# Gated linear attention: the state carried over tiles of 128 frames, decays measured from the middle of a tile

## The chip, the cores and the metric

The kernel runs on one core of one Trainium2 chip. The metric is device time of one execution, in microseconds. A core has five engines that run beside each other and meet at semaphores: TensorE (PE) multiplies matrices and writes to PSUM; its weight loads are shown apart, as PEld. VectorE (DVE) and ScalarE (ACT) do elementwise work and read PSUM. GpSimd (POOL) does small elementwise work here and issues DMAs, also those that add to their target. SyncE (SP) issues most weight loads.

## The reference

One layer over 512 frames of 1024 channels: three branches of the normalised input, merged by gates, an output product, and an MLP. The change touches the first branch alone, the gated linear attention (GLA) with four heads of 64 key and 128 value channels, in chunks of 64 frames:

```python
b = jnp.cumsum(log_a.reshape(B, N, CHUNK, H, DK).astype(f32), axis=2)
e_pos = jnp.exp(b)
e_neg = jnp.exp(-b)
q_pos = qc * e_pos
a_causal = jnp.einsum('bnthd,bnshd->bnhts', q_pos, kc * e_neg)
a_anti = jnp.einsum('bnthd,bnshd->bnhts', qc * e_neg, kc * e_pos)
attn = jnp.where(lower, a_causal, a_anti)
o_intra = jnp.einsum('bnhts,bnshv->bnthv', attn, vc)
chunk_kv = jnp.einsum('bnshd,bnshv->bnhdv', kc * jnp.exp(b_last - b), vc)
chunk_decay = jnp.exp(b_last[:, :, 0])
...
def step(state, inp):
    kv, dec = inp
    return state * dec[..., None] + kv, state
...
o_inter = jnp.einsum('bnthd,bnhdv->bnthv', q_pos, prev)
return (o_intra + o_inter).reshape(B, S, H, DV).astype(v.dtype)
```

A frame reads every frame of its own chunk, with a decay by the distance in time, and all earlier chunks through a state that decays channel by channel. Only differences of `b` enter the result, so `b` may be counted from any point.

## The kernel before

**Layout.** Frames are cut into NT = 4 tiles of P = 128, so a tile holds two chunks. Two heads share one group of 128 partitions: head h = 2j + e sits in the 64 rows of half e of pair j. The queries qpos, qneg are zero in the other half, so a score matmul over all 128 rows gives one head.

**Products.** The large products split each fp32 operand into a rounded part and a remainder and add three products; that is `mm3`, lines 155 to 157. A weight tile is loaded by SyncE, rounded by ScalarE (`whi`, L145), its remainder is made on VectorE (`wlo`, L146). Where a weight is the sum of two, a POOL DMA adds the second to the first (L940 in the gate stage, L130 and L132 for sums kept in DRAM, which wait for a cast that paces them). The GLA's own products are plain fp32.

**Order.** The order of TensorE is written by hand: `weave` runs a list of GLA steps and deals 64 steps of other products between them (the output gates `gla_g`, the late fox gates `fox_late`), three matmuls of 512 columns each. The list is decays, key_turn, gla_scores, states, gla_scores, gla_values twice, then the second pair of heads, with gla_turn for the finished heads. The other engines' order is made by a planner that times the program.

**GLA step by step, for a pair j.**
- `decays` (L741): four matmuls of the log decays with `tri64`, a triangle inside each chunk, give `b` in PSUM. VectorE takes each chunk's last column (`bl`) and subtracts it (`ek`); ScalarE makes four exponentials: `ek`, `ep`, `en`, `dec`. VectorE makes kd = k·ek first, then kp, qpos, kn, qneg.
- `key_turn` (L770): four transposes of kd. Rows of even chunks go to kdE (VectorE), of odd chunks to kdO (ScalarE); the other halves are zero, from two memsets on POOL.
- `states` (L778): per chunk and head a matmul of 64 columns of kdE or kdO with the values, 16 in two PSUM banks; the two heads of a chunk use the two column halves of the array. VectorE scans over seven states.
- `gla_scores` (L798): eight matmuls per head, then eight copies under a mask (`msk_s`: same chunk and s ≤ t; same chunk and s > t) into `at`, which POOL sets to zero before.
- `gla_values` (L811): per head and tile the scores with the values, 128 columns (L818), and per chunk the queries with the state before the chunk, 64 columns (L824). In the first tile the scores' product is cut into two of 64 columns (L822). Then the norm of the head.
- `gla_turn` (L835): four transposes, times the output gate.

**Behind it** the gate products (`gate_group`) run, whose left factors are sums made by `lefts_2` (x at L920 and L921, then f2h and f2l at L922 and L923), and whose results are added into `ct` by `vec` (L949).

Of the kernel before, what the change touches and what calls it, by code (L numbers as in the profile page):

```python
# [9 lines left out]
F32 = mybir.dt.float32  # L10
# [54 lines left out]
def hybrid_block(ctx, tc, chunks, wst, memT, xN, cols, gffn, gfin, wup, cst, out):  # L65
    nc = tc.nc
# [5 lines left out]
    def nm(s):  # L72
        uid[0] += 1
        return f"{s}_{uid[0]}"
# [13 lines left out]
    def at_(shape=None):  # L88
        return pa.tile(shape or [P, 512], F32, tag="a", name=nm("a"))
# [161 lines left out]
    with pool("front") as fp:  # L251
# [101 lines left out]
        for k in range(KT):  # L353
# [3 lines left out]
            if k in (3, 5):  # L357
                h = k // 5
# [366 lines left out]


    with pool("gla") as lp:
        NC = 8
        qpos = [lp.tile([P, S], F32, name=f"qpos{e}") for e in range(2)]
        qneg = [lp.tile([P, S], F32, name=f"qneg{e}") for e in range(2)]  # L730
        kdE = lp.tile([P, NT, P], F32, name="kdE")
        kdO = lp.tile([P, NT, P], F32, name="kdO")
# [5 lines left out]
        nc.gpsimd.memset(kdO[0:64], 0.0)  # L738
        gs = {}

        def decays(j):  # L741
            pb = at_()
            for t in range(NT):
                nc.tensor.matmul(pb[:, t * P:(t + 1) * P], la[:, t, j * P:(j + 1) * P], tri64, start=True, stop=True)
            ep = lp.tile([P, S], F32, tag="ep", name=nm("ep"))
            en = lp.tile([P, S], F32, tag="en", name=nm("en"))
            bl = small(lp, NC, "bl").rearrange("p (c o) -> p c o", o=1)
            dec = small(lp, NC, "dec")
            ek = lp.tile([P, NC, 64], F32, tag="ek", name=nm("ek"))
            pb3 = pb.rearrange("p (c t) -> p c t", c=NC)  # L750
# [4 lines left out]
            nc.scalar.activation(en, pb, AF.Exp, scale=-1.0)  # L755
# [3 lines left out]
            kd = lp.tile([P, S], F32, tag="kd", name=nm("kd"))  # L759
            kd_ins = nc.vector.tensor_tensor(kd, gkT[j], ek.rearrange("p c t -> p (c t)"), op=ALU.mult).ins  # L760
            with tc.issue_after(kd_ins):
                nc.vector.tensor_tensor(kn, gkT[j], en, op=ALU.mult)
                nc.vector.tensor_tensor(kp, gkT[j], ep, op=ALU.mult)
                for e in range(2):
                    a = slice(64 * e, 64 * e + 64)
                    nc.vector.tensor_tensor(qpos[e][a], gqT[j][a], ep[a], op=ALU.mult)
                    nc.vector.tensor_tensor(qneg[e][a], gqT[j][a], en[a], op=ALU.mult)
            gs["d", j] = dec, kn, kp, kd

        def key_turn(j):  # L770
            kd = gs["d", j][3]
            pk = at_([P, NT, P])
            for t in range(NT):
                nc.tensor.transpose(pk[:, t, :], kd[:, t * P:(t + 1) * P], ident)
            nc.vector.tensor_copy(kdE[0:64], pk[0:64])
            nc.scalar.copy(kdO[64:128], pk[64:128])

        def states(j):  # L778
            dec = gs["d", j][0]
            prev = gs["s", j] = lp.tile([P, NC, P], F32, tag="prev", name=nm("prev"))  # L780
            for g in range(2):
                pv = at_([P, 4, P])
                for i in range(4):
                    c = 4 * g + i
                    t = c // 2
                    for e in range(2):
                        h = 2 * j + e
                        nc.tensor.matmul(pv[64 * e:64 * e + 64, i, :], (kdO if c % 2 else kdE)[:, t, 64 * e:64 * e + 64],
                                         gv[:, t, h * P:(h + 1) * P], start=True, stop=True)
                for i in range(4):  # L790
                    c = 4 * g + i
                    if c == 0:
                        nc.vector.tensor_copy(prev[:, 1, :], pv[:, 0, :])
                    elif c < NC - 1:
                        nc.vector.scalar_tensor_tensor(prev[:, c + 1, :], prev[:, c, :], dec[:, c:c + 1], pv[:, i, :],
                                                       op0=ALU.mult, op1=ALU.add)

        def gla_scores(h):  # L798
            j, e = divmod(h, 2)
            _, kn, kp, _ = gs["d", j]  # L800
            pc, pn = at_([P, NT, P]), at_([P, NT, P])
            at = gs["a", h] = lp.tile([P, NT, P], F32, tag="at", name=nm("at"), bufs=2)
            nc.gpsimd.memset(at, 0.0)
            for m, (ps, kk, qq) in enumerate(((pc, kn, qpos[e]), (pn, kp, qneg[e]))):
                for t in range(NT):
                    sl = slice(t * P, (t + 1) * P)
                    nc.tensor.matmul(ps[:, t, :], kk[:, sl], qq[:, sl], start=True, stop=True)
                for t in range(NT):
                    nc.vector.copy_predicated(at[:, t, :], msk_s[:, m, :], ps[:, t, :])

        def gla_values(h):  # L811
            j, e = divmod(h, 2)
            at, prev = gs["a", h], gs["s", j]
            po = at_([P, NT, P])
            for t in range(NT):
                vt = gv[:, t, h * P:(h + 1) * P]
                if t:
                    nc.tensor.matmul(po[:, t, :], at[:, t, :], vt, start=True, stop=False)  # L818
                for c in (2 * t, 2 * t + 1):
                    r = slice(64 * (c % 2), 64 * (c % 2) + 64)  # L820
                    if t == 0:
                        nc.tensor.matmul(po[r, t, :], at[:, t, r], vt, start=True, stop=c == 0)  # L822
                    if c:
                        nc.tensor.matmul(po[r, t, :], qpos[e][:, 64 * c:64 * c + 64], prev[:, c, :], start=False,  # L824
                                         stop=True)
# [578 lines left out]
def layout(inputs):  # L1404
# [3 lines left out]
    x = np.asarray(inputs["x"])[0]  # L1408
# [3 lines left out]
    for i, c in enumerate(chunks):  # L1412
# [4 lines left out]
        elif c[0] == "B":  # L1417
            _, q, h, (kh, ch) = c
            j = 8 * q + 4 * h + int(kh) - 1
# [9 lines left out]
        elif c[0] == "F":  # L1429
            _, q, h, (kh, ch) = c  # L1430
            ks = slice(512 * (int(kh) - 1), 512 * int(kh))
            for n in range(2):
                j = 8 * q + 4 * h + 2 * n + int(ch) - 1
# [4 lines left out]
        else:  # L1438
            g = wst[i].reshape(P, KT, P)
# [58 lines left out]
```

## Time and profile before

| | us |
|---|---|
| median of the runs | 843.53 |
| the runs | 843.0, 843.53, 901.48 |
| span of the profiled execution | 841.1 |
| ScalarE busy, whole span | 461.6 (55%) |
| DMA moved | 155.61 MB, mean 185 GB/s |

The profile is of one execution; its span runs from the first instruction to the last, and the run's time has what lies around it as well. Busy time is the share in which an engine holds an instruction: matmuls are pipelined, so a row's length on TensorE is longer than its step, and the start of the next row tells what it cost. An idle engine costs nothing as long as another is what the end waits for.

### The profile page before, as it was taken

What the parts mean: (1) busy time and instruction counts of PE and PEld (TensorE: products, weight loads), DVE (VectorE), ACT (ScalarE), POOL (GpSimd) and SP (SyncE); (2) the same over time, 40 slices, a digit from 0 to 9 for tenths busy, and PEclk for the clock granted to TensorE, in tenths of its full rate; (3) what the DMA queues carried; (4) which work ended last, traced back from release to release, by engine and by line L of the source; (5) the groups of instructions that cost most, each with busy time, mean ns of one, the idle gap of its engine ahead of it and who ended that gap; (6) DMA issues with size and microseconds to landing.
All of it is one profiled execution on the core that took longest, in us unless ns stands there. A gap on an engine that the chain in (4) does not pass through costs nothing.

```text
span 841.1 us, 12612 instructions
## 1 busy us (share of the span) xinstructions
PE 824.4 (98%) x4841; PEld 720.5 (86%) x4841; DVE 612.4 (73%) x954; ACT 461.6 (55%) x723; POOL 106.5 (13%) x129
## 2 busy tenths in 40 slices
PE   8999999999999999999999999999999999999995
PEld 6788888888888787988999889998998899889984
DVE  4856888665565686894686757896689678877897
ACT  6765777553345232543345435875577467646754
POOL 1001000001002110131431300011001100110011
PEclk9999999999999999999999999999999999999998
DMA  9424444448779582689986522968857975895543
GB/s 332 173 100 162 154 137 150 124 145 217 214 251 250 151 250 69 161 214 273 250 215 214 181 79 63 289 179 201 246 181 166 220 234 173 186 248 196 151 86 115
DMA packets 39181, 155.61 MB, mean 185 GB/s; under 512 B 4880, under 2 KB 5840, under 8 KB 37072
## 3 DMA queue, kind: packets, MB, share of 16 engines
q1 hardware_dynamic: 27712, 95.54, 31.9%
q0 software_dynamic: 9328, 54.01, 30.6%
q10 hardware_dynamic: 2080, 5.26, 1.8%
q8 instruction: 38, 0.62, 0.3%
q14 instruction: 23, 0.19, 0.1%
HBM read 152.65 MB, written 31.49 MB: 219 GB/s over the span
## 4 chain that ended last, share of the span: by engine, by line
PE 50%; DVE 2%; DMA 2%; issue 1%; ACT 0%; POOLq 0%; POOL 0%; ACTq 0%
PE mm L157 13%; PE mm L156 13%; PE mm L155 13%; PE a L156 4%; PE a L155 4%; PE a L157 4%; DMA wb<-in_wst_dram 2%; DVE h L1168 1%; PE a L1115 0%; DVE wlo L146 0%; ACT whi L145 0%; DVE h L1295 0%; DVE lo L209 0%; DVE h L1292 0%; DVE R L1165 0%
## 5 line engine op out<-in xcount | busy, mean ns | idle before, releaser
L155 PE MATMUL mm<-uhi,whi 128*128 128x512 f32 (+1 forms) x352 | 127.0, 361 | 0.8 <-ACT whi L145 0.8
L157 PE MATMUL mm<-uhi,wlo 128*128 128x512 f32 (+1 forms) x352 | 124.8, 354 | 1.0 <-DVE wlo L146 1.0
L156 PE MATMUL mm<-ulo,whi 128*128 128x512 f32 (+1 forms) x352 | 124.3, 353 | 0.0
L146 DVE TENSOR_TENSOR wlo<-raw,whi 128x1024 fp32r<-128x1024 f32 x68 | 91.5, 1349 | 34.7 <-ACT whi L145 34.4
L145 ACT CAST whi<-raw 128x1024 fp32r<-128x1024 f32 x68 | 71.2, 1049 | 65.1 <-PE mm L156 39.0
L208 ACT CAST hi<-raw 128x1024 fp32r<-128x1024 f32 x65 | 68.2, 1050 | 47.4 <-PE mm L156 34.3
L209 DVE TENSOR_TENSOR lo<-raw,hi 128x1024 fp32r<-128x1024 f32 x65 | 79.5, 1223 | 18.6 <-ACT hi L208 18.6
L157 PEld LDWEIGHTS mm<-uhi,wlo 128*128 128x128 f32 x352 | 67.2, 191 | 10.5 <-DVE wlo L146 1.4
L155 PEld LDWEIGHTS mm<-uhi,whi 128*128 128x128 f32 x352 | 67.4, 192 | 10.2 <-ACT whi L145 1.2
L156 PEld LDWEIGHTS mm<-ulo,whi 128*128 128x128 f32 x352 | 67.4, 192 | 8.0
L208 ACT CAST hi<-b 128x1024 fp32r<-128x1024 f32 x40 | 41.9, 1048 | 41.4 <-PE mm L157 26.8
L157 PE MATMUL mm<-u2h,lo 128*128 128x256 f32 x224 | 63.4, 283 | 0.0
L156 PE MATMUL mm<-u2l,hi 128*128 128x256 f32 x224 | 63.4, 283 | 0.0
L156 PE MATMUL mm<-lo,ch 128*128 128x512 f32 x160 | 62.5, 391 | 0.9 <-DVE lo L209 0.9
L155 PE MATMUL mm<-u2h,hi 128*128 128x256 f32 x224 | 63.4, 283 | 0.0
L157 PE MATMUL mm<-hi,cl 128*128 128x512 f32 x160 | 62.3, 389 | 0.0
L155 PE MATMUL mm<-hi,ch 128*128 128x512 f32 x160 | 62.3, 389 | 0.0
L209 DVE TENSOR_TENSOR lo<-b,hi 128x1024 fp32r<-128x1024 f32 x40 | 48.8, 1222 | 18.2 <-ACT hi L208 18.2
L1352 POOL DMA_DIRECT2D b<-in_wst_dram x32 | 27.4, 855 | 272.4 <-DVE lo L209 209.3
L155 PE MATMUL mm<-u2sh,hi 128*128 128x256 f32 x168 | 47.5, 283 | 0.0
L156 PE MATMUL mm<-u2sl,hi 128*128 128x256 f32 x168 | 47.5, 283 | 0.0
L157 PE MATMUL mm<-u2sh,lo 128*128 128x256 f32 x168 | 47.5, 283 | 0.0
(413 smaller groups left out, 2156.3 us busy)
## 6 DMA issues: line engine op xcount, KB each, us to landing
raw<-in_wst_dram SPq DMA_DIRECT2D x114, 512.0 KB
b<-in_wst_dram POOLq DMA_DIRECT2D x32, 512.0 KB, 5.4
raw<-T SPq DMA_DIRECT2D x28, 512.0 KB
T<-in_wst_dram POOLq DMA_DIRECT2D x12, 1024.0 KB, 8.9
b<-in_wst_dram SPq DMA_DIRECT2D x16, 512.0 KB
wb<-in_wst_dram POOLq DMA_DIRECT2D x15, 512.0 KB, 5.9
wb<-in_wst_dram SPq DMA_DIRECT2D x8, 512.0 KB
T<-in_wst_dram POOLq DMA_DIRECT2D x6, 512.0 KB, 5.2
```

Source lines behind the costliest of these rows:

```text
L145: cast = nc.scalar.copy(hi, raw)
L146: low_now[0] = nc.vector.tensor_tensor(lo, raw, f(hi), op=ALU.subtract).ins
L155: nc.tensor.matmul(ps, lh, rh, start=start, stop=False)
L156: nc.tensor.matmul(ps, lh, rl, start=False, stop=False)
L157: nc.tensor.matmul(ps, ll, rh, start=False, stop=stop)
L208: nc.scalar.copy(hi, src)
L209: return nc.vector.tensor_tensor(lo, src, f(hi), op=ALU.subtract).ins
L1168: nc.vector.tensor_tensor(to, to, x, op=op)
L1352: nc.gpsimd.dma_start(to[i], wst[index["B", q, i, x]], accum_op=ALU.add)
```

## The change

The state is now kept at the middle of each tile of 128 frames instead of the start of each chunk of 64. `b` is counted from frame 63 of a tile, backwards and forwards; column 63 of the product, which would be zero, is used for the sum from the tile's start to its middle. With the next tile's such sum, the last column gives the decay from one middle to the next (`end`, `dec`). The exponentials of both signs are written into one tile `ex`, and POOL sets column 63 of both to 1. kn now serves the scores and the states; kd, ek, kdE and kdO are gone. The first mask covers the whole tile (s ≤ t), so the scores of a tile's second chunk with its first one are read in `at`; the states are read per tile. The matmuls of the scores are as before.

```diff
-    ident, ones, tri, tri64 = (cst_s[:, i * P:(i + 1) * P] for i in range(4))
+    ident, ones, tri, mids = (cst_s[:, i * P:(i + 1) * P] for i in range(4))
...
-        nc.gpsimd.memset(kdE[64:128], 0.0)
-        nc.gpsimd.memset(kdO[0:64], 0.0)
...
-            nc.vector.tensor_copy(bl, pb3[:, :, 63:64])
-            nc.vector.tensor_tensor(ek, pb3, bl.to_broadcast([P, NC, 64]), op=ALU.subtract)
-            nc.scalar.activation(ek, ek, AF.Exp, scale=-1.0)
+            nc.scalar.activation(en, pb, AF.Exp, scale=-1.0)
+            nc.vector.tensor_copy(end, pb3[:, :NT - 1, P - 1:])
+            nc.vector.tensor_tensor(end, end, pb3[:, 1:, 63:64], op=ALU.add)
             nc.scalar.activation(ep, pb, AF.Exp)
-            nc.scalar.activation(en, pb, AF.Exp, scale=-1.0)
-            nc.scalar.activation(dec, bl.rearrange("p c o -> p (c o)"), AF.Exp)
+            nc.scalar.activation(dec, end.rearrange("p c o -> p (c o)"), AF.Exp)
+            nc.gpsimd.memset(ex.rearrange("p i t c -> p (i t) c")[:, :, 63:64], 1.0)
...
-            kd_ins = nc.vector.tensor_tensor(kd, gkT[j], ek.rearrange("p c t -> p (c t)"), op=ALU.mult).ins
-            with tc.issue_after(kd_ins):
-                nc.vector.tensor_tensor(kn, gkT[j], en, op=ALU.mult)
+            kn_ins = nc.vector.tensor_tensor(kn, gkT[j], en, op=ALU.mult).ins
+            with tc.issue_after(kn_ins):
                 nc.vector.tensor_tensor(kp, gkT[j], ep, op=ALU.mult)
...
-            for t in range(NT):
-                nc.tensor.transpose(pk[:, t, :], kd[:, t * P:(t + 1) * P], ident)
-            nc.vector.tensor_copy(kdE[0:64], pk[0:64])
-            nc.scalar.copy(kdO[64:128], pk[64:128])
+            for t in range(NT - 1):
+                nc.tensor.transpose(pk[:, t, :], kn[:, t * P:(t + 1) * P], ident)
+            kt = gs["k", j] = lp.tile([P, NT - 1, P], F32, tag="kt", name=nm("kt"))
+            nc.scalar.copy(kt, pk[:, :NT - 1, :])
...
+            for t in range(NT - 1):
+                for e in range(2):
+                    h = 2 * j + e
+                    nc.tensor.matmul(pv[64 * e:64 * e + 64, t, :], kt[:, t, 64 * e:64 * e + 64], gv[:, t, h * P:(h + 1) * P],
+                                     start=True, stop=True)
+            for t in range(NT - 1):
+                x = pv[:, t, :]
+                if t:
+                    x = mid[:, 0, :]
+                    nc.vector.tensor_tensor(x, mid[:, t, :], pv[:, t, :], op=ALU.add)
+                nc.vector.tensor_scalar(mid[:, t + 1, :], x, dec[:, t:t + 1], None, op0=ALU.mult)
...
             for t in range(NT):
-                vt = gv[:, t, h * P:(h + 1) * P]
+                nc.tensor.matmul(po[:, t, :], at[:, t, :], gv[:, t, h * P:(h + 1) * P], start=True, stop=t == 0)
                 if t:
-                    nc.tensor.matmul(po[:, t, :], at[:, t, :], vt, start=True, stop=False)
-                for c in (2 * t, 2 * t + 1):
-                    r = slice(64 * (c % 2), 64 * (c % 2) + 64)
-                    if t == 0:
-                        nc.tensor.matmul(po[r, t, :], at[:, t, r], vt, start=True, stop=c == 0)
-                    if c:
-                        nc.tensor.matmul(po[r, t, :], qpos[e][:, 64 * c:64 * c + 64], prev[:, c, :], start=False,
-                                         stop=True)
+                    nc.tensor.matmul(po[:, t, :], qpos[e][:, t * P:(t + 1) * P], mid[:, t, :], start=False, stop=True)
...
-    cst[:, 3 * P:4 * P] = np.where(same & (s <= t), 1.0 / 16.0, 0.0)
-    cst[:, 4 * P:5 * P] = same & (s <= t)
+    half = np.where(s < 64, -1.0 * (t < 63) * (s > t) + 1.0 * (t == 63), 1.0 * (s <= t) * (t > 63))
+    cst[:, 3 * P:4 * P] = half / 16.0
+    cst[:, 4 * P:5 * P] = s <= t
```

More of the change, by code (lines that the diff above doesn't have):

```diff
@@ L727, in hybrid_block @@
     with pool("gla") as lp:
-        NC = 8
         qpos = [lp.tile([P, S], F32, name=f"qpos{e}") for e in range(2)]
         qneg = [lp.tile([P, S], F32, name=f"qneg{e}") for e in range(2)]
-        kdE = lp.tile([P, NT, P], F32, name="kdE")
-        kdO = lp.tile([P, NT, P], F32, name="kdO")
         for e in range(2):
@@ L743, in decays @@
             for t in range(NT):
[L744 to L750, printed above, removed]
-            nc.vector.tensor_copy(bl, pb3[:, :, 63:64])
-            nc.vector.tensor_tensor(ek, pb3, bl.to_broadcast([P, NC, 64]), op=ALU.subtract)
-            nc.scalar.activation(ek, ek, AF.Exp, scale=-1.0)
+                nc.tensor.matmul(pb[:, t * P:(t + 1) * P], la[:, t, j * P:(j + 1) * P], mids, start=True, stop=True)
+            pb3 = pb.rearrange("p (t c) -> p t c", t=NT)
+            ex = lp.tile([P, 2, NT, P], F32, tag="ex", name=nm("ex"))
+            ep, en = (ex[:, i].rearrange("p t c -> p (t c)") for i in range(2))
+            dec = small(lp, NT - 1, "dec")
+            end = small(lp, NT - 1, "end").rearrange("p (c o) -> p c o", o=1)
+            nc.scalar.activation(en, pb, AF.Exp, scale=-1.0)
+            nc.vector.tensor_copy(end, pb3[:, :NT - 1, P - 1:])
+            nc.vector.tensor_tensor(end, end, pb3[:, 1:, 63:64], op=ALU.add)
             nc.scalar.activation(ep, pb, AF.Exp)
-            nc.scalar.activation(en, pb, AF.Exp, scale=-1.0)
-            nc.scalar.activation(dec, bl.rearrange("p c o -> p (c o)"), AF.Exp)
+            nc.scalar.activation(dec, end.rearrange("p c o -> p (c o)"), AF.Exp)
+            nc.gpsimd.memset(ex.rearrange("p i t c -> p (i t) c")[:, :, 63:64], 1.0)
             kn = lp.tile([P, S], F32, tag="kn", name=nm("kn"))
             kp = lp.tile([P, S], F32, tag="kp", name=nm("kp"))
-            kd = lp.tile([P, S], F32, tag="kd", name=nm("kd"))
-            kd_ins = nc.vector.tensor_tensor(kd, gkT[j], ek.rearrange("p c t -> p (c t)"), op=ALU.mult).ins
-            with tc.issue_after(kd_ins):
-                nc.vector.tensor_tensor(kn, gkT[j], en, op=ALU.mult)
+            kn_ins = nc.vector.tensor_tensor(kn, gkT[j], en, op=ALU.mult).ins
+            with tc.issue_after(kn_ins):
                 nc.vector.tensor_tensor(kp, gkT[j], ep, op=ALU.mult)
@@ L767, in decays @@
                     nc.vector.tensor_tensor(qneg[e][a], gqT[j][a], en[a], op=ALU.mult)
-            gs["d", j] = dec, kn, kp, kd
+            gs["d", j] = dec, kn, kp
         def key_turn(j):
-            kd = gs["d", j][3]
+            kn = gs["d", j][1]
             pk = at_([P, NT, P])
-            for t in range(NT):
-                nc.tensor.transpose(pk[:, t, :], kd[:, t * P:(t + 1) * P], ident)
-            nc.vector.tensor_copy(kdE[0:64], pk[0:64])
-            nc.scalar.copy(kdO[64:128], pk[64:128])
+            for t in range(NT - 1):
+                nc.tensor.transpose(pk[:, t, :], kn[:, t * P:(t + 1) * P], ident)
@@ L778, in states @@
+            kt = gs["k", j] = lp.tile([P, NT - 1, P], F32, tag="kt", name=nm("kt"))
+            nc.scalar.copy(kt, pk[:, :NT - 1, :])
         def states(j):
[L779 to L796, printed above, removed]
+            dec, kt = gs["d", j][0], gs["k", j]
@@ new lines, in states @@
+            mid = gs["s", j] = lp.tile([P, NT, P], F32, tag="mid", name=nm("mid"))
+            pv = at_([P, NT, P])
+            for t in range(NT - 1):
[9 more added lines that the diff above has]
+                nc.vector.tensor_scalar(mid[:, t + 1, :], x, dec[:, t:t + 1], None, op0=ALU.mult)
@@ L798, in gla_scores @@
         def gla_scores(h):
             j, e = divmod(h, 2)
-            _, kn, kp, _ = gs["d", j]
+            _, kn, kp = gs["d", j]
             pc, pn = at_([P, NT, P]), at_([P, NT, P])
@@ L812, in gla_values @@
             j, e = divmod(h, 2)
-            at, prev = gs["a", h], gs["s", j]
+            at, mid = gs["a", h], gs["s", j]
             po = at_([P, NT, P])
             for t in range(NT):
-                vt = gv[:, t, h * P:(h + 1) * P]
+                nc.tensor.matmul(po[:, t, :], at[:, t, :], gv[:, t, h * P:(h + 1) * P], start=True, stop=t == 0)
                 if t:
-                    nc.tensor.matmul(po[:, t, :], at[:, t, :], vt, start=True, stop=False)
-                for c in (2 * t, 2 * t + 1):
-                    r = slice(64 * (c % 2), 64 * (c % 2) + 64)
-                    if t == 0:
-                        nc.tensor.matmul(po[r, t, :], at[:, t, r], vt, start=True, stop=c == 0)
-                    if c:
-                        nc.tensor.matmul(po[r, t, :], qpos[e][:, 64 * c:64 * c + 64], prev[:, c, :], start=False,
-                                         stop=True)
+                    nc.tensor.matmul(po[:, t, :], qpos[e][:, t * P:(t + 1) * P], mid[:, t, :], start=False, stop=True)
             sq = lp.tile([P, NT, P], F32, tag="sq", name=nm("sq"))
```

## The prediction

> **What bounds the kernel now.** I read the page first, then the busy times by stage, the waits, and the timeline of TensorE where the diff works. In the page, PE is the matmul side of TensorE, PEld its weight loads.
>
> ```profile
> span 841.1 us, 12612 instructions
> ...
> PE 824.4 (98%) x4841; PEld 720.5 (86%) x4841; DVE 612.4 (73%) x954; ACT 461.6 (55%) x723; POOL 106.5 (13%) x129
> ```
>
> TensorE is busy for 98% of the span. That is an average, so I asked for the stages: the stretch of the gated linear attention (265 to 336 us), a part of its end, and the gate products behind it. Columns: length, busy time and instructions of PE, PEld, DVE, ACT and POOL, granted clock, share of the DMA engines, GB/s.
>
> ```profile
> 265.00:336.00 71.00, 71.00 (x450) 56.61 (x449) 48.72 (x114) 20.75 (x32) 12.59 (x19) 1.00 0.58 174
> 320.00:335.00 15.00, 15.00 (x91) 10.81 (x90) 7.67 (x21) 2.74 (x4) 2.04 (x2) 1.00 0.11 36
> 336.00:420.00 84.00, 82.03 (x549) 75.76 (x548) 59.92 (x58) 35.33 (x43) 24.60 (x23) 0.98 0.88 227
> ```
>
> In the attention's stage PE is never idle, VectorE is busy for 49 of 71 us and ScalarE for 21. So here the end is set by how long TensorE needs for its list, which is written out by hand, and a shorter list should shorten the kernel. In the list stand the attention's matmuls between 64 "fill" steps of gate projections (L155 to L157). But busy is not work. The waits of the weight loads in the same stage show gaps that no other engine causes ("issue"; total, times, longest):
>
> ```profile
> PEld a L818 <- issue: 1.7, 10, 0.2
> PEld a L822 <- issue: 1.4, 4, 0.4
> ```
>
> Both lines are in gla_values. The timeline of its first head shows what they are (start, length, engine, line, shape, count):
>
> ```profile
> 288.37 0.39 PE L157 MATMUL mm<-uhi,wlo 128*128 128x512 f32 x1
> 288.69 0.44 PE L822 MATMUL a<-gv,at 128*64 128x128 f32 x4
> 288.96 0.38 PE L824 MATMUL a<-prev,qpos 128*64 128x128 f32 x2
> 289.28 0.49 PE L818 MATMUL a<-gv,at 128*128 128x128 f32 x2
> 289.69 0.44 PE L824 MATMUL a<-prev,qpos 128*64 128x128 f32 x4
> 290.06 0.49 PE L818 MATMUL a<-gv,at 128*128 128x128 f32 x2
> ...
> 291.27 0.44 PE L824 MATMUL a<-prev,qpos 128*64 128x128 f32 x4
> 291.64 0.50 PE L155 MATMUL mm<-uhi,whi 128*128 128x512 f32 x1
> ```
>
> Each fp32 matmul has two records. The shape changes between 64 columns (128\*64) and 128 at every row, and the two records of L818 take 0.41 us to the next start. The scores, all of one shape, show the price without changes:
>
> ```profile
> 284.52 0.39 PE L157 MATMUL mm<-uhi,wlo 128*128 128x512 f32 x1
> 284.75 1.05 PE L807 MATMUL a<-qpos,kn 128*128 128x128 f32 x8
> 285.64 1.06 PE L807 MATMUL a<-qneg,kp 128*128 128x128 f32 x8
> 286.45 0.47 PE L155 MATMUL mm<-uhi,whi 128*128 128x512 f32 x1
> ```
>
> Eight matmuls (16 records) from 284.75 to 286.45: 0.21 us each, half of L818's price.
>
> **The output step (gla_values), four heads.** Before, a head takes 291.64 - 288.69 = 2.95 us for twelve matmuls. After, it has seven, all 128 wide, in one shape with the fills and scores around them: 7 x 0.21 = 1.49 us. Less: 1.46. The step into it goes too: from the last fill to the first output matmul 0.32 us (288.37 to 288.69), into the scores 0.23 (284.52 to 284.75): 0.09. Per head 1.55, for four heads 6.2 us, all on the path.
>
> Here the Trainium skill is weighed. "TensorEngine Tiling (Array Packing)", Theoretical Speedup, promises up to 2x for operands of at most 64 columns, since column tiles work side by side; by that alone the change mostly gives the packing up, and the four heads would save an estimated 0.4 us. Its Key Properties add that a change of tiling mode drains TensorE, without a price. The trace agrees with both: narrow pairs do run together, and the 0.2 us behind L818 is the drain's size, so I keep 6.2.
>
> **The states, two head pairs.**
>
> ```profile
> 280.65 0.44 PE L788 MATMUL a<-gv,kdE 128*64 128x128 f32 x4
> 280.92 0.39 PE L788 MATMUL a<-gv,kdO 128*64 128x128 f32 x4
> 281.13 0.39 PE L788 MATMUL a<-gv,kdE 128*64 128x128 f32 x4
> ...
> 282.54 0.50 PE L155 MATMUL mm<-uhi,whi 128*128 128x512 f32 x1
> ```
>
> Eight chunks, each 0.22 us for the two heads (280.92 to 281.13), 1.89 in all. Three tiles remain, still 64 wide: 5 x 0.22 = 1.1 us less, 2.2 for both pairs. The change of shape on the way in and out stays.
>
> **The key turns.**
>
> ```profile
> 274.86 0.60 PE L774 MATMUL a<-cst_s,kd 128*128 128x128 f32 x4
> 275.21 0.48 PE L155 MATMUL mm<-uhi,whi 128*128 128x512 f32 x1
> ```
>
> Four transposes in 0.35 us become three: 0.09 less, 0.2 for both. Sum on TensorE: 6.2 + 2.2 + 0.2 = 8.6 us.
>
> **VectorE and ScalarE lose work** (the difference to a chunk's end, kd, the copy to kdE, seven state operations for five, one exponential), none of it on the path, as PE waits for none of it: worth nothing. **The new wait** is on POOL. Column 63 of the exponentials is set to 1 by a memset, and kn, now the first product, waits for it; the key turn, the scores and the states wait for kn. In the built order each memset stands behind the issue of a paced DMA (L132). The second decay step of before, the tighter one, bounds it:
>
> ```profile
> 303.29 0.58 POOL L132 DMA_DIRECT2D T<-in_wst_dram  x1 [3.71 <-ACT whi L145]
> 303.91 0.59 ACT L755 ACTIVATE en<-a 128x512 f32<-128x512 f32 x1
> 304.17 0.69 DVE L760 TENSOR_TENSOR kd<-gkT,ek 128x512 f32<-128x512 f32 x1
> 307.39 1.38 DVE L767 TENSOR_TENSOR qneg<-gqT,en 64x512 f32<-64x512 f32 x2
> 308.42 0.60 PE L774 MATMUL a<-cst_s,kd 128*128 128x128 f32 x4
> 310.94 1.05 PE L807 MATMUL a<-qpos,kn 128*128 128x128 f32 x8
> 267.50 0.52 POOL L738 MEMSET kdO<- 64x512 f32 x1
> ```
>
> The first row of kd (304.17, 0.69 long) ends 3.6 us before its transposes start, the last factor (307.39 + 1.38 = 308.8) 2.2 us before its scores. The fills between them do not change. The new chain is longer by at most one exponential (0.59), one DMA issue (0.58) and one memset (at most the 0.52 of a far larger one): 1.7 us, inside both covers. Price between 0 and, if the DMA's cast comes one weight tile later, about 3 us; I take 0, as the cast that paces it stands ahead of the second exponential in ScalarE's new order. POOL also loses two memsets ahead of the first paced DMA. The DMA queues of SyncE keep their order.
>
> **What may be late next.** TensorE stays full through the stage: the output products' norms feed turns that stand the same fills away. For the last head the built order puts one 0.7 us product ahead of the norm's scaling on VectorE, which leaves about nothing over; 0 to 0.2 us. In the gate stage the planner has changed VectorE's order: f2l (L923) comes behind both ct operations of L949 instead of between them, and the sum it is made from comes one cast remainder later. A row of the timeline, then three waits from 255 us on (total, times, longest):
>
> ```profile
> 359.58 0.68 DVE L949 TENSOR_TENSOR ct<-ct,mm 128x512 f32<-128x512 f32 x1
> PEld mm L156 <- DVE f2l L923: 0.6, 1, 0.6
> ACT whi L145 <- DMA wb<-in_wst_dram: 26.0, 7, 7.4
> PEld mm L155 <- ACT whi L145: 1.2, 1, 1.2
> ```
>
> TensorE already waits 0.6 us for f2l there. One more ct (0.68) ahead of it, and a copy of the same size that now precedes a weight cast on ScalarE and partly fills a wait, make it 0.6 to 1.1 us worse. I take 0.9, and nothing more for the last head. Net: 8.6 - 0.9 = 7.7 us.
>
> **Rivals.**
>
> *The gaps stay.* If the 0.41 us of L818 belongs to a matmul that adds to a bank and not to the change of shape, only the count matters: the states' rows show two narrow matmuls in 0.22 us beside each other, the price of one wide one, so a head's nine narrow and three wide were worth 7.5 wide and become 7, 0.5 x 0.21 x 4 = 0.4 us. With the states and turns 0.4 + 2.4 - 0.9 = 1.9 us: 841.6. For it: no run here has a 128-wide fp32 accumulation without changes. Against: the same gap stands where a narrow group meets a fill (291.27 to 291.64, for two pairs). Chance 0.07.
>
> *Given back to the transfers.* In the gate stage the DMA engines are 88% busy and ScalarE waits 26 us for loads, 1.2 of which reach PE. If those loads had a clock of their own, the 7.7 us would come back there: 841 to 843.5. Against: from 320 to 335 us the DMA share is 0.11, so the loads behind it are released by the work, and come earlier with it. Chance 0.08.
>
> *The memset comes late.* POOL waited 3.71 us for a cast ahead of L132. By the queue depths in "TensorE: Matmul & The Clock Gate" of the Trainium skill, Architectural detail, GpSimd works strictly in order; the trace agrees, as nothing passes that wait. If the memset sits behind such a wait for one weight tile, TensorE stands about 3 us at the second key turn and under 1 at the first: 836 + 3.5 = 839.5. Chance 0.05.
>
> *Slower.* Two of the seven load waits become visible. Seven times in the gate stage a whi cast waits for an accumulating load, up to 7.4 us, nearly all hidden. The new order moves casts and f2l there; if this pushes the next accumulation behind a 1 MB sum in the POOL queue twice, the path gains up to 2 x 7.4 = 14.8 us, against 8.6 saved: about 850. It decides from 8.6 us of new waiting on. For it: the stage has little room. Against: the queue's order is unchanged, and a move of under 1 us is a tenth of what it needs. Chance 0.04.
>
> **How the numbers follow.** The span of 841.1 us lies 2.4 under the median of the three runs, 843.53 (843.0 to 901.48); I take what lies around the span as fixed. 843.5 - 7.7 = 835.8. The forecast has 0.76. Its own range: all 8.6 kept and the 1.2 us wait gone too, 833.7; the losses doubled and noise of half a microsecond, 837.5. To hold the time 8 times in 10 I reach up past the late memset to 840.5, which leaves out 0.19. Two per cent, about what a measurement of this kernel tells from no change, is 16.9 us: faster than 826.7 would need twice the sum, 0.01; slower than 860.4 is beyond even the slower rival's price, 0.02; within, 0.97.
>
> **What would show it.** Right: rows of gla_values with one shape, about 1.5 us from the first to the next fill; the states near 0.8 us; no waits of PE on kn, at or mid; the attention's end about 8.5 us earlier, and all behind it shifted by as much, less some 0.9 us at f2l. Wrong: a wait of PE's weight loads on DVE kn behind POOL ex, matmuls of the new output step 0.4 us apart, or more waiting on whi between the gate products.

## The result, and the profile after

| | before | after |
|---|---|---|
| median of the runs, us | 843.26 (840.93 to 901.48, four) | 834.29 (832.3 to 834.9, four) |
| ratio, 95% interval | | 0.9898 (0.9878 to 0.9917) |
| profiled execution: time, span | span 841.1 | 834.9, span 833.1 |

The gain is 9.0 us, 1.0%, and clear of zero by its interval. The execution of 901.48 us, 58 us above the others of its kernel, is left out of the ratio; without it the median before is 843.0. The forecast was 835.8.

The page of the changed kernel, its span and its busy times:

```profile
span 833.1 us, 12436 instructions
...
PE 816.1 (98%) x4759; PEld 717.4 (86%) x4759; DVE 606.8 (73%) x946; ACT 459.8 (55%) x721; POOL 105.4 (13%) x129
```

TensorE has 82 matmul records less and is busy 8.3 us less: the same share of a shorter span. Where the time went shows in three stretches: from the first decay matmul to the last `gla_turn`, from there to the first mixing matmul (the gate stage), and the rest. Busy times by stretch of the kernel before, then of the changed one; the columns are those of the prediction's first such table.

```profile
265.79:335.81 70.02, 70.02 (x444) 55.78 (x443) 48.53 (x114) 20.75 (x32) 12.13 (x19) 1.00 0.58 173
335.81:467.49 131.68, 129.71 (x878) 120.37 (x877) 95.61 (x98) 58.53 (x72) 38.79 (x35) 0.99 0.83 219
467.49:841.10 373.61, 363.76 (x2217) 326.74 (x2215) 294.30 (x371) 225.34 (x316) 36.10 (x42) 0.99 0.64 178
```

```profile
263.77:325.01 61.24, 61.24 (x363) 52.35 (x362) 43.12 (x106) 18.98 (x30) 11.20 (x19) 1.00 0.66 198
325.01:459.47 134.46, 130.36 (x879) 120.42 (x877) 95.90 (x98) 59.09 (x73) 38.76 (x35) 0.99 0.82 214
459.47:833.10 373.63, 363.79 (x2217) 326.75 (x2215) 293.62 (x370) 224.75 (x315) 36.04 (x42) 0.99 0.66 178
```

The attention's stage is 8.78 us shorter and still full. The gate stage, of which no instruction was changed, only the planner's order, is 2.78 us longer. The rest is the same to 0.02 us. And the stage begins 2.02 us earlier, ahead of any changed instruction: 8.78 + 2.02 - 2.78 = 8.02, the 8.0 us between the spans. Whether those 2.02 and 2.78 us belong to the change needed more profiles.

The states of a pair and the first head of `gla_values` after (timeline of TensorE: start, length, engine, line, shape, count):

```profile
278.49 0.88 PE L779 MATMUL a<-gv,kt 128*64 128x128 f32 x12
279.30 0.50 PE L155 MATMUL mm<-uhi,whi 128*128 128x512 f32 x1
...
285.12 0.40 PE L157 MATMUL mm<-uhi,wlo 128*128 128x512 f32 x1
285.35 0.61 PE L806 MATMUL a<-gv,at 128*128 128x128 f32 x4
285.79 0.39 PE L808 MATMUL a<-mid,qpos 128*128 128x128 f32 x2
286.02 0.39 PE L806 MATMUL a<-gv,at 128*128 128x128 f32 x2
...
286.69 0.39 PE L808 MATMUL a<-mid,qpos 128*128 128x128 f32 x2
286.83 0.48 PE L155 MATMUL mm<-uhi,whi 128*128 128x512 f32 x1
```

The gaps inside a head are gone, as all its matmuls have one shape: 286.83 - 285.35 = 1.48 us a head. The states, first two rows, take 0.81 us for a pair.

The gate stage after. First the waits of TensorE there (total, times, longest), then their places in its timeline:

```profile
PE mm L157 <- DVE wlo L146: 1.7, 3, 0.8
PE mm L155 <- ACT whi L145: 1.4, 1, 1.4
PE mm L156 <- DVE f2l L906: 0.9, 1, 0.9
```

```profile
350.39 0.39 PE L155 MATMUL mm<-f2h,whi 128*128 128x256 f32 x1
351.72 0.39 PE L156 MATMUL mm<-f2l,whi 128*128 128x256 f32 x1 [0.94 <-DVE f2l L906]
...
409.83 0.28 PE L156 MATMUL mm<-f2l,whi 128*128 128x256 f32 x1
409.95 0.28 PE L157 MATMUL mm<-f2h,wlo 128*128 128x256 f32 x1
411.62 0.38 PE L155 MATMUL mm<-f1h,whi 128*128 128x256 f32 x1 [1.39 <-ACT whi L145]
411.84 0.28 PE L156 MATMUL mm<-f1l,whi 128*128 128x256 f32 x1
412.88 0.38 PE L157 MATMUL mm<-f1h,wlo 128*128 128x256 f32 x1 [0.76 <-DVE wlo L146]
...
413.38 0.42 PE L157 MATMUL mm<-f1h,wlo 128*128 128x256 f32 x1
413.60 0.42 PE L155 MATMUL mm<-f1h,whi 128*128 128x256 f32 x1
```

A step of 256 columns takes 0.12 us (409.83 to 409.95). What a step takes beyond that is the wait: 1.2 us for f2l, 1.6 for whi at 411 us, 0.9 for wlo behind it. Counted so over the whole stage, TensorE waited 2.6 us before and 5.3 after: +2.7, which is the 2.78.

The last two rows stand 0.22 us apart and not 0.12. From 413.3 to 416.6 us the granted clock was 0.50, on both sides of it 1.00. The trace of the kernel before has such a stretch as well, from 398.6 to 401.9 us, so it is no part of the 2.78.

### The profile page after: what moved, and what is told of

Read it like the earlier page. It is cut to its first block, busy times and chain, and to the rows that moved or that the text cites. A ratio compares the mean times of both kernels' runs of the same rounds, so it can differ in the third digit from the quotient of the medians.

```text
span 833.1 us, 12436 instructions
## 1 busy us (share of the span) xinstructions
PE 816.1 (98%) x4759; PEld 717.4 (86%) x4759; DVE 606.8 (73%) x946; ACT 459.8 (55%) x721; POOL 105.4 (13%) x129
## 4 chain that ended last, share of the span: by engine, by line
PE 46%; DVE 5%; DMA 3%; issue 1%; ACT 1%; POOLq 0%; POOL 0%; ACTq 0%; DVEq 0%
PE mm L157 12%; PE mm L156 12%; PE mm L155 12%; PE a L155 3%; PE a L156 3%; PE a L157 3%; DMA wb<-in_wst_dram 3%; DVE wlo L146 1%; DVE lo L209 1%; DVE h L1151 1%; DVE cl L209 0%; PE a L1098 0%; ACT whi L145 0%; DVE ct L979 0%; DVE R L1148 0%
## 5 line engine op out<-in xcount | busy, mean ns | idle before, releaser
L157 PEld LDWEIGHTS mm<-uhi,wlo 128*128 128x128 f32 x352 | 66.6, 189 | 10.5 <-DVE wlo L146 1.4
```

The costliest lines, as they stand in the source:

```text
L157: nc.tensor.matmul(ps, ll, rh, start=False, stop=stop)
```

## The experiments

**The theories.** A: a change of shape between 64 and 128 columns costs TensorE time, whatever the matmuls do; taking these changes out made most of the gain, and part of it is given back in the gate stage to transfers. Rivals: B, the gap belongs to a matmul that adds to a bank, or to the count of matmuls; C, the waits of the gate stage are a matter of chance or of one tile's own chain, and not of what else is loaded; D, the memset costs something.

All spans of the three stretches, in us, from the same three places in each trace:

| kernel | start of the stage | attention's stage | gate stage | time, median (runs) | ratio to before (interval) |
|---|---|---|---|---|---|
| before | 265.79 | 70.02 | 131.68 | 843.26 (4) | |
| b_again | 264.37 | 70.02 | 131.74 | 841.55 (1) | |
| after | 263.77 | 61.24 | 134.46 | 834.29 (4) | 0.9898 (0.9878 to 0.9917) |
| a_again | 263.46 | 61.24 | 133.22 | 835.30 (6) | 0.9911 (0.9891 to 0.9931) |
| e1_mid_halves | 264.29 | 65.32 | 133.19 | 837.22 (6) | 0.9939 (0.9917 to 0.996) |
| e2_all_halves | 263.68 | 62.46 | 133.42 | 834.27 (6) | 0.9902 (0.9883 to 0.9921) |
| e4_states_twice | 264.09 | 62.54 | 133.33 | 834.94 (4) | 0.9907 (0.9883 to 0.993) |
| e6_pool_3 | 263.63 | 64.15 | 131.57 | 836.82 (4) | 0.9922 (0.9899 to 0.9945) |
| e3_f2l_first | 263.85 | 61.24 | 133.22 | 834.33 (6) | 0.9905 (0.9885 to 0.9926) |
| e7_sums_later | 264.31 | 61.24 | 128.54 | 830.44 (6) | 0.9864 (0.9838 to 0.989) |
| e7_again | 264.68 | 61.24 | 128.54 | 830.62 (4) | 0.9851 (0.9833 to 0.9868) |
| b_sums_later | 264.16 | 70.03 | 127.75 | 840.90 (12) | 0.9977 (0.9964 to 0.9989) |
| e8_both | 264.79 | 61.24 | 128.54 | 830.65 (4) | 0.985 (0.983 to 0.987) |
| e9_f2_sum_early | 266.77 | 61.24 | 127.22 | 830.84 (4) | 0.985 (0.9815 to 0.9885) |

**Both kernels once more (a_again, b_again).**

> The changed kernel once more, beside the others on the same chip. If the gain is TensorE's shorter list, the attention's stage (first decay matmul to the last turn) takes 61.2 us again, against 70.0 before, and the whole is 7 to 9 us faster. Two waits for weights behind it are open: 2.5 us for an accumulated load some 86 us after the last turn, and 2.0 us less at the start of the program than in the profile of before. If they belong to the change they come again; if they come from how loads happen to land they do not, or with another size.

> The kernel before, profiled once more, to tell which of the differences between the two traces belong to the change. The first decay matmul stood at 265.8 us before and at 263.8 and 263.5 us in two profiles of the changed kernel, ahead of any changed instruction. Theory: the loads at the start differ from run to run, so this profile may start the stage anywhere from 263 to 266 us, with the stage again 70.0 us long. Rival: the change moves the start too, then 265.8 again. Behind the stage the theory of transfers wants the same waits of TensorE as in the first profile of before, 2.6 us from 326 to 450 us (0.4 for f2l, 0.4 and 1.8 for weights), against 5.4 us in both profiles of the changed kernel.

The attention's stage came out the same to 0.01 us, 70.02 and 61.24, so single profiles can be compared there. The start of the stage lies anywhere from 263.5 to 266.8 us, with the changed kernel and a variant of it at the two ends, and 264.4 in the repeated kernel before: the 2.02 us were mostly chance. The gate stage before took 131.74 us, with 4.1 us of waits and not 2.6; after, 133.22 with 5.4. In the two first profiles TensorE's mean granted clock in this stage was 0.99, in the two repeated ones 1.00: only the first two have the stretch of 3.4 us at 0.50. Without its waits the stage took 129.1 and 129.1 against 127.7 and 127.8 us, so the stretch is worth 1.4 us. Before the change, the profile with the stretch waited 1.5 us less, so that the two stages came out alike (131.68 and 131.74). Like with like, the change costs the gate stage 1.5 us (repeated profiles) to 2.8 us (first ones).

**The shapes back, on one side (e1) and on both (e2).**

```diff
 # e1_mid_halves
-                    nc.tensor.matmul(po[:, t, :], qpos[e][:, t * P:(t + 1) * P], mid[:, t, :], start=False, stop=True)
+                    for r in (slice(0, 64), slice(64, 128)):
+                        nc.tensor.matmul(po[r, t, :], qpos[e][:, t * P + r.start:t * P + r.stop], mid[:, t, :], start=False,
+                                         stop=True)
 # e2_all_halves: the same, and
-                nc.tensor.matmul(po[:, t, :], at[:, t, :], gv[:, t, h * P:(h + 1) * P], start=True, stop=t == 0)
+                for r in (slice(0, 64), slice(64, 128)):
+                    nc.tensor.matmul(po[r, t, :], at[:, t, r], gv[:, t, h * P:(h + 1) * P], start=True, stop=t == 0)
```

> Only the three state matmuls of each head's output are cut into two of 64 columns, as narrow pairs. Changes of shape cost (theory): a head has six changes again; by the rows of before 0.44 + 0.2, then 0.37, 0.42, 0.37, 0.42, 0.37 = 2.6 us instead of 1.48, four heads +4.4 us. The number of matmuls costs (rival): three more narrow ones at the price of a wide one each, +2.5 us, with no gaps behind them. Accumulating costs and shape does not (rival): 0.

> All seven matmuls of each head's output are cut into two of 64 columns, so there are more narrow ones than in the run beside it, but one change of shape on the way in and one on the way out. Changes of shape cost (theory): about 0.1 in and 0.16 out, four heads +1.0 us, less than the run with three cut. The number of matmuls costs (rival): seven more, +5.9 us, more than that run. Accumulating costs (rival): 0.

TensorE's timeline in a head of e1, then of e2:

```profile
285.64 0.40 PE L157 MATMUL mm<-uhi,wlo 128*128 128x512 f32 x1
285.88 0.60 PE L806 MATMUL a<-gv,at 128*128 128x128 f32 x4
286.41 0.44 PE L809 MATMUL a<-mid,qpos 128*64 128x128 f32 x4
286.78 0.49 PE L806 MATMUL a<-gv,at 128*128 128x128 f32 x2
...
288.36 0.50 PE L155 MATMUL mm<-uhi,whi 128*128 128x512 f32 x1
```

```profile
285.02 0.40 PE L157 MATMUL mm<-uhi,wlo 128*128 128x512 f32 x1
285.35 0.66 PE L807 MATMUL a<-gv,at 128*64 128x128 f32 x8
285.84 0.39 PE L810 MATMUL a<-mid,qpos 128*64 128x128 f32 x4
286.06 0.39 PE L807 MATMUL a<-gv,at 128*64 128x128 f32 x4
...
287.03 0.50 PE L155 MATMUL mm<-uhi,whi 128*128 128x512 f32 x1
```

e1 changes shape six times a head and takes 288.36 - 285.88 = 2.48 us, 1.00 more than after: 0.17 us a change. e2 has twice the matmuls of after and only two changes, on the way in and out; its pairs follow each other at 0.22 us, as whole matmuls do, and the head takes 1.68 us, with 0.1 more on the way in: 0.15 a change. So neither the number of narrow matmuls nor the adding makes the gaps (every second row of e2 adds to a bank), only the changes do: B falls. Over four heads the stage grew by 4.08 us (e1) and 1.22 (e2); the theory had 4.4 and 1.0, the count 2.5 and 5.9. The medians, which also hold the start and the gate stage, don't show it (1.9 us above a_again and 1.0 below). The price also gives the old head: eight changes of 0.167 and eight steps of 0.215 us make 3.06; it took 2.95 and 0.09 on the way in. Of the 1.56 us that a head gained, some 1.3 are changes of shape.

The Trainium skill, "TensorEngine Tiling (Array Packing)", Key Properties, says that a change of mode drains TensorE; these runs give the price of a change, and don't show that the drain is what takes the time. The "up to 2x" of its Theoretical Speedup is met in e2, two narrow matmuls in the time of one, and gains nothing here, since one wide matmul does the work of the two in the same time.

**The states (e4).** Their products are issued a second time.

```diff
-            for t in range(NT - 1):
+            for t in [t for t in range(NT - 1) for _ in range(2)]:
```

> The changed kernel with each matmul of the state products issued twice (12 in place of 6 in each pair of heads, the second over the first). Theory: TensorE sets the pace of the stage, and the six matmuls left cost 0.80 us with their entry, so the second six add 0.66 us in each pair: 1.3 us in the stage from first decay matmul to last turn (62.5 in place of 61.2) and about that in the time. Rival: the states lie beside other work, and nothing is added (61.2).

The stage took 62.54, 1.30 more than 61.24, as the theory has it. A pair of states matmuls less is 0.22 us less on the path. In the time the 1.3 us don't show (834.94 against 834.29 and 835.30): the gate stage was 1.1 us shorter than in the first profile of the changed kernel, 0.9 of it at f2l (below).

**The memset late (e6).** Sums that nobody uses, on GpSimd ahead of each memset.

```diff
+            scr = lp.tile([P, S], F32, tag="scr", name=nm("scr"))
+            for _ in range(3):
+                nc.gpsimd.tensor_tensor(scr, ep, en, op=ALU.add)
             nc.gpsimd.memset(ex.rearrange("p i t c -> p (i t) c")[:, :, 63:64], 1.0)
```

> The changed kernel with three sums of 128x512 (unused, some 1.3 to 1.6 us each by the rows of GpSimd in the gate stage) on GpSimd ahead of each memset of the column of the middle, so that the memset, and the key factor behind it, come some 4.5 us later. The covers measured in the changed kernel are 5.0 us at the first key turn and 2.9 us at the second. Theory (the wait for GpSimd costs nothing because it ends within these covers, and would cost what goes beyond them): no wait of TensorE at the first key turn, about 1.6 us (1 to 2) at the second, in the stage 62.2 to 63.3 us in place of 61.2. Rival 1 (the cover is larger than it looks, the scheduler's order leaves slack elsewhere): stage 61.2. Rival 2 (the sums also slow VectorE through what the two engines share): DVE rows beside them longer, wait beyond 2 us.

In the changed kernel itself the memset took 0.11 us and kn waited 0.8 us for it, long ahead of the key turn at 272.84 us. The wait (total, times, longest) and the memset's row in the timeline of GpSimd:

```profile
DVE kn L753 <- POOL ex L750: 0.8, 1, 0.8
```

```profile
267.04 0.11 POOL L750 MEMSET ex<- 128x8 f32 x1 [0.76 <-ACT ex L748]
```

In e6 the memset came 4 us later; the timeline of GpSimd and VectorE, and TensorE's wait:

```profile
270.99 0.11 POOL L753 MEMSET ex<- 128x8 f32 x1
271.08 1.23 DVE L146 TENSOR_TENSOR wlo<-raw,whi 128x1024 fp32r<-128x1024 f32 x1 [4.87 <-ACT whi L145]
272.22 0.68 DVE L834 SCALAR_TENSOR_TENSOR sg<-tt,mm 128x512 f32<-128x512 f32 x1
272.82 0.68 DVE L756 TENSOR_TENSOR kn<-gkT,ex 128x512 f32<-128x512 f32 x1
...
301.44 1.78 DVE L209 TENSOR_TENSOR og<-og,og 128x512 fp32r<-128x512 f32 x1 [0.69 <-ACT og L208]
```

```profile
PE a L769 <- DVE kn L756: 2.5, 2, 1.7
```

The expectation missed: TensorE waited at both key turns (1.0 and 1.9 us by its starts), and the stage grew by 2.9 us, not by 1 to 2. At the first, kn, once late, stands behind a weight half and an output gate on VectorE (271.08 to 272.82). At the second, rival 2 has a part in it: the row of `og` at 301.44, which the order puts ahead of kn, ran beside the three sums of that turn (298.54 to 302.68) and took 1.78 us, where the changed kernel needs 0.68. A memset that comes late by 4.1 us is covered for this delay less the waits, 3.1 us at the first key turn and at least 2.3 at the second, and not for the 5.0 and 2.9 between kn's end and the key turn. D falls for the kernel as it is: 0.1 us of work, no wait of TensorE.

The gate stage of e6 was 131.57 us, 1.65 less than in a_again, both without the stretch at half clock. 0.7 us of that is a shorter wait for f2l (below), the rest are shorter waits for weights. That suggests that a TensorE that comes later finds the transfers further on. e7 tests that straight.

**The sums of the gate stage moved behind it (e7, and b_sums_later on the kernel before).**

```diff
-        op = next(sums, None) if (n > 23 or n > 11 and n % 2 == 0) and (n < 44 or n > 51 and n % 3 == 0) else None
+        op = next(sums, None) if (n > 23 or n > 11 and n % 2 == 0) and (n < 44 or n > 79) else None
```

> The last six sums of weight blocks (the T transfers of L130 and L132, 1 MB each, which share the queue with the weights of the gate stage at 358 to 428 us) are issued after the gate stage, at some 457 to 482 us, where the transfer engines were a third to two thirds busy. Theory (what the shorter attention stage gained is partly given back to transfers in the gate stage): the weight waits of TensorE at 386 to 388 and 411 to 413 us (0.2 + 0.9 and 1.6 + 0.9 us, of which 3.0 to 3.6 us in three profiles) go, all but the 0.36 at 364 us, and the time falls by 2.5 to 3.6 us against the changed kernel: ratio to before 0.986 to 0.987. Rival: those waits come from the chain of load, accumulated load and cast of one tile alone, whatever else is in flight: they stay within 0.5 us and the time with them.

> The same move of the six sums in the kernel before. Its weight waits from 326 to 450 us were 0.4 + 0.9 + 0.9 = 2.2 us. Theory of transfers: they go too, and the time falls by some 1.8 us, less than the 2.5 to 3.6 us of the changed kernel, so that with the transfers out of the way the change is worth 9 to 10 us less 1 us for f2l. Rival (the waits are a matter of one tile's own chain): time as before, within 0.5 us.

> e7_sums_later once more, beside e8_both on one chip. Theory of transfers: no wait of TensorE for weights from 360 to 450 us, and 3 to 5 us under the changed kernel's 834.3 to 835.3 us.

The busy times of the gate stage of e7_again, and the one kind of wait of its matmuls left there:

```profile
325.92:454.46 128.54, 127.58 (x878) 118.80 (x877) 92.83 (x99) 59.38 (x74) 35.95 (x31) 1.00 0.71 179
```

```profile
PE mm L156 <- DVE f2l L906: 0.9, 1, 0.9
```

All waits for weights are gone, also the 0.36 us that were expected to stay, and the stage is 4.7 us shorter than in a_again. By the medians e7 is 3.7 to 4.9 us under the changed kernel, more than the 2.5 to 3.6 first expected. The DMA share fell from 0.83 (a_again) to 0.71. The accumulated load (L923) behind the wait at 411 us, first in the changed kernel, then three of them in e7_again:

```profile
L923 POOL DMA_DIRECT2D wb<-in_wst_dram x1: 884/884/884, 401.1 to 401.1; - x1
DMA to landing us min/median/max: 9.3/9.3/9.3
```

```profile
L923 POOL DMA_DIRECT2D wb<-in_wst_dram x3: 860/880/1209, 398.3 to 406.9; - x3
DMA to landing us min/median/max: 5.3/5.3/8.5
```

A 512 KB accumulation that took 9.3 us beside a sum of 1 MB takes 5.3 in its place without it (the first of the three; the 8.5 is one of two issued together). C falls. Whether the accumulations wait for each other in GpSimd's queue or in the transfer engines, these runs don't tell. With 830.4 and 830.6 us this is the fastest kernel of the study, together with e8 and e9, which keep the move, and 12 us under the kernel before beside it. In the kernel before, the same move took 4.0 us from the gate stage, but 3.3 came back in the two stretches behind it, to the first product of the MLP and some 44 us on (46.10 to 47.78 and 43.52 to 45.10 us), and the time fell by 1.9. The expected 1.8 was right for the time and not for the way; why those stretches lose more there than in e7 (0.5 and 0.2 us) wasn't followed.

With the transfers out of the way the gate stage is 0.8 us longer after the change than before it (128.54 and 127.75). That is f2l: 0.7 us in these two traces. Between these two kernels the change is worth 10.5 us (840.90 to 830.44): 8.8 in the attention's stage, less 0.8, and the 2.5 by which the stretches behind differ.

**The wait for f2h and f2l (e3, e8, e9).** The prediction had put it down to two ct operations ahead of f2l and to the sum it is made from. e3 issues the ct operations of product 6 behind f2l; e8 and e9 move sums, both on top of e7.

```diff
 # e3_f2l_first (the rest of the gate group as it was)
-            take(6, product(6, w))
+                with tc.issue_after(left_low[0]):
+                    take(6, p6)
 # e9_f2_sum_early, in the first lefts_2, behind f1l; the second leaves it out
+                if then is not None:
+                    nc.vector.tensor_tensor(xsum[1], then, xsum[1], op=ALU.subtract)
```

> In the first gate group the two ct operations of product 6 are put behind the remainder f2l on VectorE; the rest is the changed kernel. If the planner's new order gave back part of the gain there (theory), TensorE's 1.4 us of waiting for f2h and f2l falls to 0.4 or less and the whole is 1.0 us faster. If the loads of the gate stage set the pace (rival), the waits for accumulated loads behind it grow by as much and the time is the same.

> The changed kernel with the late sums as in e7_sums_later, and with the two block sums that f2h and f2l are made of (L903, L904) issued right behind f1l, ahead of the two weight halves on VectorE, and no longer behind them. Theory (the 0.2 + 1.2 us wait of TensorE for f2h and f2l at 350 to 352 us is a matter of that queue on VectorE): the wait falls under 0.3 us and the time by 1.1 to 1.4 us against e7_sums_later. Rival 1 (the two sums push the weight halves wlo at 343 to 348 us, and TensorE waits there instead): 0 to -0.5 us. Rival 2 (the cast f2h waits for its tile, not for the sum): no change.

> e7_sums_later, and the first of the two block sums that f2h and f2l are made of (L903) issued right behind f1l, so that the second (L904) takes its place on VectorE and the cast f2h and f2l come some 2.3 us earlier. (The move in e8_both had taken the sums of f1, which were early enough.) Theory (the 0.2 + 1.2 us wait of TensorE for f2h and f2l is the queue on VectorE: two weight halves wlo and two ct sums ahead of f2l): the wait of 1.4 us goes, or falls under 0.3 us, and the time by 1.1 to 1.4 us against 830.5 us: 829.1 to 829.4. Rival 1 (a weight half wlo, pushed back by the sum, becomes the wait): waits of 0.2 to 1 us at 343 to 348 us and a time within 0.5 us of 830.5. Rival 2 (the cast f2h waits for its tile): f2l wait as before, 830.5.

VectorE's timeline in the changed kernel, in e3 and in e9, and the busy times of e9's gate stage:

```profile
345.71 2.35 DVE L146 TENSOR_TENSOR wlo<-raw,whi 128x1024 fp32r<-128x1024 f32 x2
347.98 1.22 DVE L904 TENSOR_TENSOR x<-x,ulo 128x1024 f32<-128x1024 f32 x1
...
350.44 1.22 DVE L906 TENSOR_TENSOR f2l<-x,f2h 128x1024 fp32r<-128x1024 f32 x1
```

```profile
350.65 1.22 DVE L906 TENSOR_TENSOR f2l<-x,f2h 128x1024 fp32r<-128x1024 f32 x1 [1.17 <-ACT f2h L905]
```

```profile
348.71 1.22 DVE L905 TENSOR_TENSOR x<-x,ulo 128x1024 f32<-128x1024 f32 x1
349.85 1.22 DVE L146 TENSOR_TENSOR wlo<-raw,whi 128x1024 fp32r<-128x1024 f32 x1
```

```profile
328.01:455.23 127.22, 127.22 (x878) 118.86 (x877) 92.03 (x99) 59.48 (x74) 35.92 (x31) 1.00 0.73 182
```

In e3 VectorE now idles 1.17 us for the cast f2h, and f2l comes no earlier: the ct operations cost nothing. (Its median is 1.0 us under that of a_again, as the theory wanted, but equal to the first one of the changed kernel, and its gate stage is that of a_again, 133.22.) What is late is the sum x (L904), which the planner puts behind both weight halves; before the change it stood between them. In e1, e2, e4 and e6 the planner's order came out with x between them again, and TensorE waited 0.5 to 0.7 us for f2l, as before the change (0.4 and 0.7), and not the 1.4 for f2h and f2l of the changed kernel. e8 was meant to move this sum, but moved those of f1, which had time, and changed nothing. e9 puts x ahead of the second half again, and TensorE then waits for nothing in the whole gate stage (127.22 of 127.22 us busy). The 1.3 us it gains there come back behind in this profile: waits for weights among the mixing products, by the starts 0.4 us at that place in e7_again, are 1.8 us, the stretch to the first product of the MLP takes 48.05 us and not 46.62, and the median is that of e7. The profile is of the slowest of four executions (829.6 to 832.8 us), so what the wait is worth in the two at 829.6 and 829.7 isn't shown.

## Why the prediction was right

- **The output step** (6.2 us for four heads): 4 x (2.95 - 1.48 + 0.09) = 6.2. e1 and e2 show the mechanism: 0.15 to 0.17 us a change of shape.
- **The states** (2.2): 2 x (1.89 - 0.81) = 2.2; e4 shows that it lies on the path. **The key turns** (0.2): 0.35 to 0.24 us, two of them. The sum of 8.6 was 8.78 in the stage.
- **The memset at nothing**: right, TensorE never waited for it. At the second key turn the prediction had 3.6 us of cover, less at most 1.7 of a longer chain; the rows give 2.9, and e6 at least 2.3. That a late kn also loses its place on VectorE was not foreseen.
- **f2l** (0.9 us, from 0.6 to 1.1): 0.7 to 1.0. The size was right by luck. It was priced with one more ct operation and a copy on ScalarE. The ct costs nothing (e3), and behind the copy ScalarE idles 3.7 us for x in the changed kernel. The later sum, which the prediction names and gives no price, is the cause.
- **The transfers** were the term left at zero. The step "if those loads had a clock of their own ... Against: ... the loads behind it are released by the work, and come earlier with it" holds only in part: some 0.7 to 1.8 us came back as waits for weights (1.5 to 2.8 of the gate stage, less f2l). The rival's full 7.7 did not: with the sums of the gate stage alone moved, all these waits go. How much came back is uncertain, as the waits for weights in two profiles of the kernel before differ by 1.2 us.
- **Net.** By the repeated profiles 8.78 - 1.48 = 7.3 us, by the medians 9.0 and 7.5, against the predicted 7.7. The spans also hold 0.9 to 2.0 us from the start of the program, which varies by itself: that the first median came within 1.5 us of the forecast is partly chance.
- **Readings.** The gap from 291.27 to 291.64 us, put down to "two pairs", belongs to one pair (four records are two matmuls); two pairs at 0.22 us each would leave no gap, one leaves 0.15. TensorE "already waits 0.6 us for f2l" is the wait of its weight loads; by the starts of the matmuls it was 0.4. The upper end of its own range adds to 837.2 and not 837.5.

## What to carry to other kernels

Count the changes of tile shape in TensorE's list before the matmuls: at 0.15 to 0.17 us each they were worth more than the matmuls saved. Where the stage behind a shortened one keeps its DMA engines busy, as here for 0.82 to 0.84 of the time, ask whether part of the gain comes back as waits for loads, and look for a transfer there that can go later. A wait that is free by the distance between two rows may cost more once late, because in an engine's order others step ahead. And a mean clock of 0.99 may be one stretch at half speed: look for it before comparing two profiles.

## What the runs showed of the hardware

Two 64-column fp32 matmuls beside each other take 0.22 us, as one of 128 columns, also when they add to a bank. The stage without loads on its path repeats to 0.01 us over seven profiles, of the changed kernel and of variants that leave it alone, while the start of the program varied by 3.3 us (263.46 to 266.77). A subtraction of two tiles on VectorE that takes 0.68 us took 1.78 beside a sum on GpSimd (e6).

The clock granted in the gate stage was not lower by a hundredth, as its mean says, but 0.50 for one stretch of 3.4 us, worth 1.4 us. Five profiles have it there (before, after, e1, e2, e4), each time behind two waits of TensorE for weights that add to 1.8 to 2.5 us; in b_again, a_again, e3 and e6 two such waits of 1.6 to 2.1 us left the clock alone. In the five with the sums moved, which have no such waits, the clock of this stage stayed at 1.00. The late start of e9 (266.77 us) has a stretch at 0.50 as well, from 24.8 to 28.2 us.
